# Low parts of the projection weights on VectorE instead of GpSimd, in two stages of a hybrid decoder block

## The chip, the cores and the metric

The kernel runs on one core of one Trainium2 chip. The metric is the device time of one execution in microseconds (us), the median of several runs. Besides, one execution is profiled: its trace has every instruction of the five engines, TensorE (PE; its weight loads are listed apart as PEld), VectorE (DVE), ScalarE (ACT), GpSimd (POOL) and SyncE (SP, which issues most DMAs).

## The reference, cut to what matters

One layer of a decoder block on 1024 tokens behind 16 learned ones, model width 1024, in float32:

```python
u = rmsnorm(h, norm1_w[l]) @ w_in[l]
(a_q, a_k, a_v, a_gate, a_b, a_a, b_z, b_xbc, b_dt, c_q, c_k, c_v, gate_logits) = split_in(u)
y_gdn = gdn_branch(a_q, a_k, a_v, a_gate, a_b, a_a, ...)   # gated delta rule, 8 heads of 128
y_ssd = ssd_branch(b_z, b_xbc, b_dt, ...)                  # state space, 4 groups, chunks of 128
y_swa = swa_branch(c_q, c_k, c_v, swa_sinks[l])            # windowed attention
merged = g_a * (y_gdn @ w_proj_gdn[l]) + g_b * (y_ssd @ w_proj_ssd[l]) + g_c * (y_swa @ w_proj_swa[l])
h = h + merged @ w_out[l]
h = h + jnp.square(jax.nn.relu(rmsnorm(h, norm2_w[l]) @ w_up[l])) @ w_down[l]
```

`q`, `k`, `v` of the delta net and `x`, `b`, `c` of the state space pass a short causal convolution along the tokens and a SiLU. The delta net then solves a triangular system in each chunk and carries a state from chunk to chunk.

## The kernel before, in words

**Numbers in two parts.** A float32 operand of a large product is split into a high part, a copy rounded to the type `fp32r`, and a low part, the difference of the number and its high part. A product is three passes over the contraction: high by high, high by low, low by high.

**A projection.** `proj` (line 174) computes 128 columns of `w_in` against all tokens. `split_w` (line 119) gets the weight tile: a DMA on SyncE's queue brings 128x1024 numbers into `wr`; ScalarE copies them into `wh` (line 124); GpSimd subtracts, `wl = wr - wh` (line 126, one instruction on 128x1024). `gemm` then runs, for each of two or three chunks of tokens, eight products `wh` by `hnh`, eight `wh` by `hnl` and eight `wl` by `hnh` (line 150). So `wl` is needed only in the last third of a chunk. `wr`, `wh` and `wl` have two buffers each: the tile for one projection is made while the one before it is multiplied, and it can be written only when the product two tiles earlier is over. In the trace `wl` bears the projection's name: `kl`, `vl`, `ql`, `ggl` in the delta net, `xl`, `zl`, `bl`, `cl` in the state space.

**The stages.** `stage_norm` (to about 32 us), `stage_gdn` (the delta net, to 640 us, some 79 us for each of 8 heads), `stage_ssd` (the state space, to 1060 us, some 100 us for each of 4 groups), `stage_swa` (attention), then gates, the merge of the branches, the output projection and the MLP.

**What VectorE does in the delta net.** The convolution of `q`, `k`, `v` (one step on line 354, three on line 359, two closing ones on line 362 behind ScalarE's tanh); the solve, a chain of 62 short instructions in which `xt` (line 514) and `ub` (line 516) wait for each other; the scan over the chunks, where `rr` (line 591) feeds PE's `py` (line 597) and `S` (line 609) feeds PE's `ks` (line 589); and products with decay matrices (`dm` line 479, which PE's `qtp`, line 486, waits for, since `dm` frees a bank of PSUM; `w` line 443). In the state space: the same convolutions (its first step on line 356), `xd` (line 721), `sq` (line 807, ahead of PE's `sst`, line 809), `dms` (line 777).

**What GpSimd does besides `wl`.** Selections under a diagonal (`dm` line 426, `dms` line 680), products with decays (`kt` line 448, `qt` line 470, `xw` line 726, `x` by `z` line 797) and powers for norms (lines 421, 632, 814; the last, `sf`, goes to PE's `sfr`, line 819).

**What sets the order.** Each engine works through its own queue in order, and an instruction that waits holds all behind it. The order in the queues is fixed when the program is built, by a planner that takes, of the instructions it reckons ready on an engine, the one that stands earliest in the program. `weave` and `tick` put the steps of the previous head's scan between the products of a projection in the program's text.

Of the kernel before, what the change touches and what calls it, by code (L numbers as in the profile page):

```python
# [7 lines left out]
F32 = mybir.dt.float32  # L8
# [3 lines left out]
ALU = mybir.AluOpType  # L12
# [51 lines left out]
class Trunk:  # L64
    def __init__(self, ctx, tc, I, out):
        self.ctx, self.tc, self.nc, self.I, self.out = ctx, tc, tc.nc, I, out
        nc = self.nc
        self.const = ctx.enter_context(tc.tile_pool(name="const", bufs=1))
        self.wst = ctx.enter_context(tc.tile_pool(name="wst", bufs=2))
        self.dram = ctx.enter_context(tc.tile_pool(name="scr", bufs=1, space=DRAM))  # L70
        self.pmm = ctx.enter_context(tc.tile_pool(name="pmm", bufs=3, space=PSUM))
        self.pcr = ctx.enter_context(tc.tile_pool(name="pcr", bufs=3, space=PSUM))
        self.pbx = ExitStack()
        self.open_psum()
        self.co = None
        const = self.const
        self.ident = const.tile([P, P], F32, name="ident")
        make_identity(nc, self.ident)
        self.tri = const.tile([P, P], F32, name="tri")
        nc.gpsimd.memset(self.tri, 1.0)  # L80
        nc.gpsimd.affine_select(out=self.tri, in_=self.tri, compare_op=ALU.is_ge, fill=0.0,
                                base=0, pattern=[[1, P]], channel_multiplier=-1)
        self.ones = const.tile([P, 1], F32, name="ones")
        nc.gpsimd.memset(self.ones, 1.0)
        self.pneg = const.tile([P, 16], F32, name="pneg")
        nc.gpsimd.memset(self.pneg, -0.5)
        self.ppos = const.tile([P, 16], F32, name="ppos")
        nc.gpsimd.memset(self.ppos, 0.5)
        self.cols = const.tile([P, NCOL], F32, name="cols")
        nc.scalar.dma_start(self.cols, I["cols"])  # L90
        self.hnw = const.tile([P, 9], F32, name="hnw")
        nc.vector.tensor_scalar(self.hnw, self.cols[:, C_GNW:C_GNW + 9], 0.5, None, op0=ALU.mult)
        self.hdk = const.tile([P, 8], F32, name="hdk")
        nc.vector.tensor_scalar(self.hdk, self.cols[:, C_DSK:C_DSK + 8], 0.5, None, op0=ALU.mult)
        self.sink = const.tile([P, SH], F32, name="sink")
        nc.scalar.dma_start(self.sink, I["sinks"].broadcast_to([P, SH]))
        self.yd = [self.dram.tile([KT, P, SEQ], F32, name=f"yd{b}") for b in range(3)]
        self.gad = self.dram.tile([3 * KT, P, SEQ], F32, name="gad")
        self.acd = self.dram.tile([NPR, 7, P, 512], F32, name="acd")
        self.xd = self.dram.tile([HOIST, P, 512], F32, name="xd")  # L100
        self.hd = self.dram.tile([NB, P, D], F32, name="hd")
        self.rowd = self.dram.tile([32, NC, P], F32, name="rowd")
        self.ald = self.dram.tile([32, NC], F32, name="ald")
        self.frd = self.dram.tile([SG, NB, P], F32, name="frd")
# [14 lines left out]
    def split_w(self, src, name):  # L119
        nc = self.nc  # L120
        wr = self.wst.tile([P, KT, P], F32, name=name + "r", tag="wr")
        nc.sync.dma_start(wr.rearrange("p k c -> p (k c)"), src)
        wh = self.wst.tile([P, KT, P], F32R, name=name + "h", tag="wh")
        nc.scalar.activation(wh, wr, AF.Copy)  # L124
        wl = self.wst.tile([P, KT, P], F32R, name=name + "l", tag="wl")
        nc.gpsimd.tensor_tensor(wl, wr, wh.bitcast(F32), op=ALU.subtract)  # L126
        return wh, wl

    def half(self, tag, bufs, name, dt=F32R, pool=None):
# [1516 lines left out]
def build(ctx, tc, I, out):  # L1646
    k = Trunk(ctx, tc, I, out)
    nc = tc.nc
    pool = lambda st, name, **kw: st.enter_context(tc.tile_pool(name=name, **{"bufs": 1, **kw}))
    ph, ps, px = ExitStack(), ExitStack(), ExitStack()  # L1650
    k.px = ExitStack()
    k.pa = ExitStack()
    with nc.allow_non_contiguous_dma(reason="layout"):
        k.tp = pool(ctx, "tp")
        k.hn = pool(ph, "hn", side="right")
        k.c2 = pool(k.pa, "c2")
        k.sp = pool(ps, "smp", side="right")
        k.xp = pool(px, "xp", side="right", bufs=3)
        k.stage_norm()
        px.close()  # L1660
        k.open_branches()
        cur = k.gdn_first()
        k.stage_small()
        ps.close()
        k.open_gdn()
        k.stage_gdn(cur)
        k.open_rest()
        k.stage_ssd()
        k.open_psum()
        store = k.stage_swa()  # L1670
        k.gates = {}
        k.merge_gates(0, (0, 1))
        w2 = k.gate_w(0, 2)
        store()
        k.px.close()
        k.pa.close()
        k.pbx.close()
        k.pdr = pool(ctx, "pdr", space=PSUM, reuse_waits="tile")
        k.lp = pool(ctx, "lp", reuse_waits="tile")
        k.ph, k.py = ph, ExitStack()  # L1680
        k.stage_merge(w2)
        k.py.close()
        k.rp = pool(ctx, "rp", side="right", reuse_waits="tile")
        k.stage_out()
        k.stage_mlp()
    return k
# [73 lines left out]
```

## Time and profile before

| | us |
|---|---|
| median of 3 runs | 2650.71 (2644.99 to 2651.49) |
| the profiled execution | 2650.12 |
| its span, first to last instruction | 2648.40 |
| busy in the span: PE | 2507.6 (95%) |
| VectorE | 1754.3 (66%) |
| ScalarE | 1071.5 (40%) |
| GpSimd | 572.2 (22%) |

A busy PE is not PE at its peak, since its instructions are pipelined and their ends modelled. "PEclk" in the tables is the clock that PE was granted, as a share of 2.4 GHz. In an instruction's row the number behind the start is its duration; the brackets say how long its engine was idle before it and what ended that. Several like instructions in a row are merged (x2, x8).

### The profile page before, as it was taken

What the parts mean: (1) busy time and instruction counts of PE and PEld (TensorE: products, weight loads), DVE (VectorE), ACT (ScalarE), POOL (GpSimd) and SP (SyncE); (2) the same over time, 40 slices, a digit from 0 to 9 for tenths busy, and PEclk for the clock granted to TensorE, in tenths of its full rate; (3) what the DMA queues carried; (4) which work ended last, traced back from release to release, by engine and by line L of the source; (5) the groups of instructions that cost most, each with busy time, mean ns of one, the idle gap of its engine ahead of it and who ended that gap; (6) DMA issues with size and microseconds to landing.
All of it is one profiled execution on the core that took longest, in us unless ns stands there. A gap on an engine that the chain in (4) does not pass through costs nothing.

```text
span 2648.4 us, 37818 instructions
## 1 busy us (share of the span) xinstructions
PE 2507.6 (95%) x13863; PEld 2142.1 (81%) x13863; DVE 1754.3 (66%) x3267; ACT 1071.5 (40%) x2647; POOL 572.2 (22%) x471
## 2 busy tenths in 40 slices
PE   6999999999999999999998999999999999999998
PEld 5887888888888989878887887888877788878886
DVE  5786678677457656567777754454537777686878
ACT  4334444343423323356554433221246454444443
POOL 3322222222223323321220000222341000041230
PEclk9999899999999999999999999999999999999999
DMA  3211111111111121231211334544234544666422
GB/s 117 74 37 54 54 54 54 46 53 41 61 62 59 65 77 67 62 84 49 69 61 64 134 109 136 187 159 159 92 116 155 198 166 149 214 232 206 147 87 97
DMA packets 136952, 271.84 MB, mean 103 GB/s; under 512 B 41302, under 2 KB 41718, under 8 KB 136766
## 3 DMA queue, kind: packets, MB, share of 16 engines
q1 hardware_dynamic: 131214, 256.94, 28.9%
q0 software_dynamic: 4544, 11.14, 1.7%
q8 instruction: 109, 1.79, 0.3%
q10 hardware_dynamic: 1008, 1.34, 0.2%
q14 instruction: 77, 0.63, 0.1%
HBM read 196.34 MB, written 66.59 MB: 99 GB/s over the span
## 4 chain that ended last, share of the span: by engine, by line
PE 72%; DVE 18%; issue 3%; DMA 3%; ACT 2%; POOL 1%; SPq 0%; ACTq 0%; DVEq 0%; POOLq 0%
PE dn L1540 10%; PE pr L1183 9%; PE up L1345 9%; PE gp L1103 7%; PE pso L1247 3%; PE aq L150 3%; PE x L150 3%; PE gg L150 3%; PE q L150 2%; PE v L150 2%; DVE xt L514 2%; PE z L150 2%; PE b L150 2%; PE k L150 2%; PE c L150 2%
## 5 line engine op out<-in xcount | busy, mean ns | idle before, releaser
L1540 PE MATMUL dn<-wh,ah 128*128 128x512 f32 x448 | 175.3, 391 | 4.3 <-ACT wh L1285 4.3
L1540 PE MATMUL dn<-wl,ah 128*128 128x512 f32 x448 | 175.2, 391 | 0.6 <-POOL wl L1286 0.6
L1540 PE MATMUL dn<-wh,al 128*128 128x512 f32 x448 | 175.0, 391 | 0.0
L1183 PE MATMUL pr<-yh,wph 128*128 128x512 f32 x384 | 150.2, 392 | 5.2 <-ACT yh L137 5.2
L126 POOL TENSOR_TENSOR wpl<-wpr,wph 128x1024 fp32r<-128x1024 f32 x24 | 60.0, 2501 | 420.4 <-PE gp L1103 215.3
L1183 PE MATMUL pr<-yl,wph 128*128 128x512 f32 x384 | 150.4, 393 | 0.0
L1183 PE MATMUL pr<-yh,wpl 128*128 128x512 f32 x384 | 149.8, 391 | 0.0
L1286 DVE TENSOR_TENSOR al<-ar,ah 128x512 fp32r<-128x512 f32 x112 | 99.0, 887 | 41.5 <-ACT ah L1285 41.3
L1285 ACT ACTIVATE ah<-ar 128x512 fp32r<-128x512 f32 x112 | 70.3, 627 | 108.2 <-PE dn L1540 80.8
L1286 POOL TENSOR_TENSOR wl<-wd,wh 128x512 fp32r<-128x512 f32 x48 | 71.8, 1501 | 193.3 <-ACT wh L1285 73.2
L1540 PEld LDWEIGHTS dn<-wh,ah 128*128 128x128 f32 x448 | 84.6, 189 | 22.5 <-ACT wh L1285 4.8
L1540 PEld LDWEIGHTS dn<-wl,ah 128*128 128x128 f32 x448 | 84.6, 189 | 18.6 <-POOL wl L1286 1.1
L1540 PEld LDWEIGHTS dn<-wh,al 128*128 128x128 f32 x448 | 84.5, 189 | 17.5
L1183 PEld LDWEIGHTS pr<-yh,wph 128*128 128x128 f32 x384 | 71.8, 187 | 23.2 <-ACT yh L137 7.4
L1183 PEld LDWEIGHTS pr<-yl,wph 128*128 128x128 f32 x384 | 72.0, 187 | 18.4 <-DVE yl L138 2.6
L1183 PEld LDWEIGHTS pr<-yh,wpl 128*128 128x128 f32 x384 | 72.0, 188 | 15.4
L124 ACT ACTIVATE wph<-wpr 128x1024 fp32r<-128x1024 f32 x24 | 25.4, 1060 | 142.5 <-PE pr L1183 130.6
L514 DVE TENSOR_TENSOR xt<-lb,ub 99x84 f32<-99x84 f32 (+23 forms) x248 | 78.4, 316 | 5.5
L1359 ACT ACTIVATE c<-c 128x512 f32<-128x512 f32 x64 | 40.3, 630 | 96.3 <-DVE c L1431 44.3
L1193 DVE SCALAR_TENSOR_TENSOR gt<-gt,pr 128x512 f32<-128x512 f32 x32 | 21.8, 687 | 81.4 <-PE pr L1183 81.3
L1345 PE MATMUL up<-uh,sh 128*128 128x512 f32 x256 | 69.8, 395 | 3.5 <-ACT sh L1285 3.5
L1345 PE MATMUL up<-ul,sh 128*128 128x512 f32 x256 | 70.2, 396 | 0.0
(549 smaller groups left out, 7273.0 us busy)
## 6 DMA issues: line engine op xcount, KB each, us to landing
ar<-acd SPq DMA_DIRECT2D x106, 256.0 KB
wu<-in_wup SPq DMA_DIRECT2D x37, 512.0 KB
acd<-s SPq DMA_DIRECT2D x64, 256.0 KB
gad<-gt SPq DMA_DIRECT2D x48, 256.0 KB
wpr<-in_wpr SPq DMA_DIRECT2D x24, 512.0 KB
yr<-yd SPq DMA_DIRECT2D x48, 256.0 KB
gt<-gad SPq DMA_DIRECT2D x48, 256.0 KB
acd<-c SPq DMA_DIRECT2D x48, 256.0 KB
```

The costliest lines, as they stand in the source:

```text
L124: nc.scalar.activation(wh, wr, AF.Copy)
L126: nc.gpsimd.tensor_tensor(wl, wr, wh.bitcast(F32), op=ALU.subtract)
L150: nc.tensor.matmul(ps[:, 0:n], a[:, k, :], b[k][:, c0:c0 + n], start=(i == 0 and k == 0), stop=(i == 2 and k == KT - 1))
L514: nc.vector.tensor_tensor(tv, lb[:, j:j + 1, j + 1:32].broadcast_to([3 * n_, n, m]), ub[:, 0:n, j:j + 1].broadcast_to([3 * n_, n, m]), op= ...
L1103: nc.tensor.matmul(ps, w[x][:, k * P:(k + 1) * P], self.go[p, k][y], start=(j == 0 and k == 0), stop=(j == 2 and k == 3))
L1183: nc.tensor.matmul(ps, x[:, k, :], y, start=(k == 0 and j == 0), stop=(k == KT - 1 and j == 2))
L1247: nc.tensor.matmul(ps, x[k, th][:, ts], y, start=(k == 0 and j == 0), stop=(k == KT - 1 and j == 2))
L1285: nc.scalar.activation(hi, src, AF.Copy)
L1286: (eng or nc.vector).tensor_tensor(lo, src, hi.bitcast(F32), op=ALU.subtract)
L1345: self.nc.tensor.matmul(ps, x[:, k * P:(k + 1) * P], ops[k][y], start=(j == 0 and k == 0), stop=(j == 2 and k == 3))
L1359: self.nc.scalar.activation(dst, src, AF.Relu)
L1540: nc.tensor.matmul(acc[t], x[:, t * P:(t + 1) * P], y, start=(i == 0 and m == 0), stop=(i == n - 1 and m == 2))
```

## The change

In the delta net and the state space (and in the first tiles, which are split in the stage of the norm) `wl` is computed by VectorE, in two instructions of 128x512, instead of by GpSimd in one of 128x1024. A flag, set when the kernel object is made and cleared ahead of `stage_swa`, chooses; from the attention on, `split_w` is as before. GpSimd keeps everything else.

```diff
@@ __init__
         self.co = None
+        self.vlo = True
@@ split_w
         wl = self.wst.tile([P, KT, P], F32R, name=name + "l", tag="wl")
-        nc.gpsimd.tensor_tensor(wl, wr, wh.bitcast(F32), op=ALU.subtract)
+        if self.vlo:
+            for k in (0, 4):
+                nc.vector.tensor_tensor(wl[:, k:k + 4, :], wr[:, k:k + 4, :], wh[:, k:k + 4, :].bitcast(F32), op=ALU.subtract)
+        else:
+            nc.gpsimd.tensor_tensor(wl, wr, wh.bitcast(F32), op=ALU.subtract)
         return wh, wl
@@ build
         k.stage_ssd()
         k.open_psum()
+        k.vlo = False
         store = k.stage_swa()
```

## Rows read from the trace of the kernel before

**Rows 1.** The page, part 4: the chain that ended last, by engine.

```profile
PE 72%; DVE 18%; issue 3%; DMA 3%; ACT 2%; POOL 1%; SPq 0%; ACTq 0%; DVEq 0%; POOLq 0%
```

**Rows 2.** Busy time of each engine by stretch (us and instructions), PE clock, DMA share, GB/s.

```profile
32.00:640.00 608.00, 562.20 (x3948) 506.01 (x3949) 422.51 (x991) 247.75 (x795) 158.75 (x111) 0.96 0.18 53
...
640.00:1060.00 420.00, 397.99 (x2518) 362.98 (x2517) 271.16 (x349) 139.81 (x348) 124.93 (x76) 0.98 0.18 63
...
1060.00:2648.40 1588.40, 1536.95 (x7353) 1264.45 (x7351) 1043.08 (x1906) 666.41 (x1478) 276.16 (x267) 0.99 0.39 131
```

**Rows 3.** PE's waits, 0 to 1060 us: total us, times, longest.

```profile
PE py L597 <- DVE rr L591: 19.3, 10, 2.6
...
PE qtp L486 <- DVE dm L479: 11.6, 5, 2.9
...
PE sst L809 <- DVE sq L807: 4.7, 3, 1.6
...
PE xtp L381 <- DVE x L362: 3.2, 2, 1.7
...
PE sfr L819 <- POOL sf L814: 3.2, 3, 1.4
```

**Rows 4.** GpSimd in order of time, 440 to 520 us: start, duration, instruction, [idle before].

```profile
474.84 2.38 POOL L126 TENSOR_TENSOR kl<-kr,kh 128x1024 fp32r<-128x1024 f32 x1 [11.03 <-PE psn L604]
...
513.46 1.56 POOL L426 TENSOR_SCALAR_AFFINE_SELECT dm<-gm 128x1024 f32<-128x1024 f32 x1
```

**Rows 5.** GpSimd in order of time, 488 to 512 us.

```profile
491.41 2.38 POOL L126 TENSOR_TENSOR vl<-vr,vh 128x1024 fp32r<-128x1024 f32 x1 [14.18 <-ACT sqo L618]
...
511.14 2.37 POOL L126 TENSOR_TENSOR ggl<-ggr,ggh 128x1024 fp32r<-128x1024 f32 x1 [0.34 <-PE k L150]
```

**Rows 6.** VectorE in order of time, 489 to 512 us.

```profile
491.53 2.36 DVE L514 TENSOR_TENSOR xt<-lb,ub 99x80 f32<-99x80 f32 x1
...
494.20 0.23 DVE L514 TENSOR_TENSOR xt<-lb,ub 99x72 f32<-99x72 f32 x1
...
494.62 0.76 DVE L354 TENSOR_SCALAR q<-qraw,cols 128x1040 f32<-128x1040 f32 x1
...
498.12 1.29 DVE L359 SCALAR_TENSOR_TENSOR q<-qraw,cols,q 128x1040 f32<-128x1040 f32 x1
...
511.53 2.53 DVE L354 TENSOR_SCALAR k<-kraw,cols 128x1040 f32<-128x1040 f32 x1
```

**Rows 7.** PE in order of time, 495 to 506 us.

```profile
499.87 0.49 PE L597 MATMUL py<-rr,w 128*128 128x128 f32 x2 [2.64 <-DVE rr L591]
```

**Rows 8.** Groups of instructions: count, busy us, mean ns, idle before.

```profile
L1286 DVE TENSOR_TENSOR wl<-T,wh 128x512 fp32r<-128x512 f32 x32 | 21.9, 684 | 6.4 <-PE dn L1540 5.9
...
L138 DVE TENSOR_TENSOR yl<-yr,yh 128x512 fp32r<-128x512 f32 x48 | 40.6, 866 | 30.0 <-ACT yh L137 29.9
...
L1286 DVE TENSOR_TENSOR wul<-wu,wuh 128x1024 fp32r<-128x1024 f32 x16 | 19.6, 1223 | 29.2 <-ACT wuh L1285 29.2
```

**Rows 9.** VectorE in order of time, 440 to 520 us.

```profile
474.87 0.35 DVE L609 SCALAR_TENSOR_TENSOR S<-S,egl,psn 128x128 f32<-128x128 f32 x1 [2.61 <-PE psn L604]
...
514.10 2.02 DVE L359 SCALAR_TENSOR_TENSOR k<-kraw,cols,k 128x1040 f32<-128x1040 f32 x1
```

**Rows 10.** VectorE in order of time, 900 to 965 us.

```profile
923.96 2.48 DVE L356 TENSOR_SCALAR x<-xraw,cols 128x1040 f32<-128x1040 f32 x1 [3.80 <-issue]
...
931.51 1.30 DVE L362 SCALAR_TENSOR_TENSOR x<-xth,x 128x528 f32<-128x528 f32 x2
...
954.62 0.82 DVE L356 TENSOR_SCALAR x<-xraw,cols 128x1040 f32<-128x1040 f32 x1 [1.04 <-DMA yd<-x]
...
960.17 2.70 DVE L362 SCALAR_TENSOR_TENSOR x<-xth,x 128x528 f32<-128x528 f32 x2 [0.71 <-ACT xth L361]
```

**Rows 11.** Busy time by stretch, around a fall of the clock.

```profile
925.00:935.00 10.00, 8.46 (x59) 8.18 (x58) 9.44 (x9) 4.78 (x10) 0.99 (x2) 1.00 0.17 54
...
935.40:945.60 10.20, 9.30 (x36) 8.85 (x36) 0.98 (x3) 0.73 (x2) 1.64 (x1) 0.50 0.08 31
```

## The prediction

> **What bounds the kernel now.** I read the chain that ended last first: TensorE (PE) has 72% of it, VectorE (DVE) 18% [rows 1]. So only what PE waits for, or what slows PE, can move the time. Then the sums by stretch: the change touches the delta net (32 to 640 us) and the state space stage (640 to 1060 us). There PE is busy 562.2 of 608 and 398.0 of 420 us; 45.8 + 22.0 = 67.8 us are idle. Its granted clock averages 0.96 and 0.98 of full speed [rows 2], which is 0.04 x 608 + 0.02 x 420 = 33 us lost at the lower clock. About 68 + 33 = 101 us is thus what this change could touch; the other 1588 us of the span keep their code.
>
> The waits of PE show who makes the idle time [rows 3]: nearly all of it ends with a VectorE instruction (the scan's right-hand side `rr` 19.3 us in 10 waits, `dm` 11.6 in 5, `sq` 4.7 in 3, the conv's last step `x` 3.2 in 2). No wait of PE in the two stages names a low part of a weight (line 126). GpSimd (POOL) makes them early enough; making them sooner is worth nothing. What can pay is what the subtraction does to VectorE.
>
> That is seen in the two engines' instructions in order of time. A subtraction on GpSimd, `kl` for one, takes 2.38 us [rows 4]. In one head of the steady state `vl` runs from 491.41 for 2.38 us [rows 5]; VectorE's `xt` that starts 0.12 us later takes 2.36 us, where the same instruction with 72 columns takes 0.23 [rows 6]. Both end together: VectorE stood for 2.13 us. `ggl` from 511.14 [rows 5] does the same to the conv's first step: 2.53 us [rows 6], against 0.76 for that instruction alone. Reading on: the conv's third weighted step runs from 498.12 [rows 6], `rr` comes behind it, and PE starts `py`, which needs `rr`, at 499.87 after 2.64 us of idle time [rows 7]. A good part of that gap is the 2.13 us that VectorE lost 6 us earlier in one unbroken run of work.
>
> **The change, part by part.** `split_w` is called 8 x 4 times for the heads and 4 x 6 times for the groups: 56 weight tiles go from GpSimd to VectorE. The switch is set back ahead of the attention stage, so 40 tiles stay as they are. No DMA moves; ScalarE's copies stay.
>
> Added to VectorE: 56 x 2 instructions of 128x512. That form exists later in the kernel, 0.684 us each with nothing beside it [rows 8], so 1.37 us a tile, 56 x 1.37 = 77 us in all.
>
> Removed from VectorE: the standing. Per head: `vl` 2.13, `ggl` 2.53 - 0.76 = 1.77; `ql` meets the same first step of the conv of `v` (I take 1.8 as for `ggl`); `kl` at 474.84 [rows 4] meets instructions that are not held up: `S` beside it takes 0.35 [rows 9]. Together 5.7 us a head against 4 x 1.37 = 5.5 us added. In a group: the first step of a conv takes 2.48 where it takes 0.82 alone, 1.66 lost; the two last steps of `x` take 2.70 where two such take 1.30 alone, 1.4 lost [rows 10]. At 1.4 a tile the six tiles lose 8.4 us against 8.2 added. Over both stages: 8 x 5.7 + 4 x 8.4 = 79 us removed, 77 added. VectorE's load does not change; what changes is when it stands and in what pieces: a piece of 2.4 us that nothing can pass becomes two of 0.68, and the queue's order is made knowing of them.
>
> What follows for PE's gaps, each with its two ends:
> - `py` behind `rr`, 10 waits, 19.3 us [rows 3]. Before, 2.13 stands ahead of `rr`. If both halves of the subtraction come ahead of it, 2.13 - 1.37 = 0.76 is won; if none does, 2.13, but no more than the gap. The low parts stand later in the program than the solve, the conv and the scan around them, so that they are filled in where nothing earlier is ready; often one half will come first. The short ones of the ten have less to give: I take 0.8 for each, 8 us (5 to 17).
> - `qtp` behind `dm`, 5 waits, 11.6 us. Before, the conv ahead of it loses 1.77 to `ggl` and 2.02 - 1.30 = 0.72 to GpSimd's `dm` selection, which queued behind `ggl` [rows 4, 6, 9]. With `ggl` gone that selection (1.56 us) moves up and may hold up the conv's start instead. So 2.49 becomes 1.37 + 0 to 1.56: from -0.4 to +1.1, and +2 where the halves come later. I take 0.6, 3 us (-2 to 9).
> - `sst` behind `sq`, 3 waits, and `xtp` behind the conv, 2 waits. 1.66 and 1.4 become 1.37 or less: 0.3 to 1.6 and 0 to 1.4. I take 0.7 each, 4 us with rounding (1 to 8).
> - Other short waits behind VectorE in these stages: 1 us (0 to 2).
>
> Together 16 us of idle time (4 to 36). The clock: after a stretch of 10 us in which PE was idle for 1.5 at full clock, 935.4 to 945.6 is granted 0.50 of full speed, 1.2 of 2.4 GHz [rows 11]; 10.2 us there do some 5 us of work. With a quarter of the idle time gone (16 of 68) I take a quarter of the 33 us: 8 us (0 to 16).
>
> What it costs: VectorE's new work where nothing was held up before, `kl` above all: 8 x 1.37 = 11 us of VectorE. At 474.84 VectorE had waited 2.61 us for PE [rows 9], so this mostly fills idle time; if that cover is gone, the scan's `S` and `rr` come 1.37 us later and PE waits. I take 3 us (0 to 11). GpSimd's shorter queue lets its other work start sooner; I count that at nothing except in the second line above. A low part that comes a few microseconds later is counted at nothing: PE waits for none now [rows 3], and if that cover is gone its waits will name the new line.
>
> Sum against the profiled execution, 2650.12 us (span 2648.40 and 1.72 around it; the median of the runs is 2650.71, 0.6 above, so they are alike): 2650.1 - 16 - 8 + 3 = 2629.
>
> One thing speaks against the sum: VectorE is busy 422.5 of 608 us in the delta net [rows 2], 69%, and GpSimd 159. If the standing that I count as removed is no gain, 77 us of work come to VectorE, and by its share of the chain (18%) [rows 1] 14 us to the time: 2664 (a rival below). The Trainium skill (Perfetto Trace Analysis, Optimizing Scalar/DVE Operations) has the rule: work may go from a saturated DVE to GpSimd, the reverse of this change; it adds that with the SBUF port they share this may not help. The 2.36 us `xt` agrees with the second half.
>
> **The rivals.**
> *Traded one for one* (about no change): all halves come ahead of whatever PE waits for, since they become ready just before the conv that they used to hold up (`ggl` 511.14, the conv's step 511.53) [rows 5, 6]. Then the idle time gives little more than its low end, 6 us, the clock nothing, and `kl` costs 4: about 2648. For it: the two sums, 79 and 77, are equal. Against it: the gaps hang on 2.13 us and 1.66 us pieces, and these shrink in any order.
>
> *VectorE waits at the head of its queue* (slower): a subtraction needs ScalarE's copy and a low buffer that PE has finished with. On GpSimd that wait harmed nobody; on VectorE the solve chain, `S`, `rr` and the conv queue behind it. The price is seen where VectorE makes low parts today: it stood 30.0 us ahead of 48 such instructions for the merge (0.63 each) and 29.2 ahead of 16 in the up projection (1.83 each) [rows 8]. At 1.2 a tile, 67 us, half of it in runs that PE waits for: +34 against -21, so 2663. It decides from 0.75 us a tile on (half of 56 x 0.75 is 21). Against it: the release is PE's last product of a projection, and the conv that follows waits for the same moment anyway; the 1.83 belongs to a stage with little else in the queue.
>
> *The block turns round*: VectorE's halves hold up what GpSimd keeps. Its `sf` is one step ahead of PE's `sfr` (3.2 us in 3 waits [rows 3]), and it makes such powers 8 + 8 + 4 times; 20 x 0.68 = 14 us less gain, about 2643. The Trainium skill (SBUF — State Buffer, Who interferes with whom) has the rule: whichever of the two starts first keeps the port for its whole instruction. The rows show only the direction in which GpSimd was first.
>
> *The load counts* (slower): the 77 us without the standing, 2664, as above. Against it: the standing is in the rows, instruction by instruction.
>
> *Gains in full*: most halves fall into idle slots, and the clock follows. 31 + 16 us off, about 2603.
>
> That the change does not do what it says can be left out: one line makes the low part, and the flag is set before the first tile.
>
> **How the numbers follow.** Forecast, 2629 with its own range 2615 to 2642: 0.50. Traded one for one, 2648: 0.20. VectorE waits at its head, 2663: 0.10. The load counts, 2664: 0.03. Turned round, 2643: 0.08. In full, 2603: 0.09. A change under 0.3% (8 us) cannot be told from none here. Faster by more: 0.50 + 0.09 + half of 0.08 + 0.03 of the trade = 0.66; within: 0.21; slower: 0.13. The range 2604 to 2656 leaves out the two slower rivals and half of the full gain, 0.18.
>
> **What would show it.** Right: in the delta net `xt` and the conv's first steps (lines 354, 356) lose their instructions above 2 us except beside GpSimd's `qt`, `dm`, `xw`; VectorE's busy time in 32 to 1060 stays within some 10 us of 693.7; PE's waits for `rr` fall from 19.3 to about 11 and for `dm` from 11.6 to about 9; the clock averages 0.97 to 0.98 in the delta net. Wrong: VectorE idle ahead of the new instructions with ScalarE or PE as releaser by more than 0.75 us a tile; or PE's waits for `rr`, `S` and `dm` unchanged in sum; or GpSimd's powers later than now. The later stages should keep their time to within 2 us; if they don't, the reason isn't in this sum.

## The result and the profile after

The change makes the kernel faster: 2601.16 us (median of 4 runs) against 2650.0 (also 4) of the kernel before, a ratio of 0.9817 with a 95% interval of 0.9801 to 0.9833, 49 us. The direction was forecast, the size was not: 2629 was predicted, and 2601 lies below the low end of the range, 2604. All ratios leave out executions at a much lower granted clock: one of experiment 4, the profiled one of experiment 9 (0.745), whose trace is therefore not read, and one of the kernel before.

The page of the kernel after, part 1 (busy us, share of the span, instructions); its profiled execution took 2595.83 us, span 2594.1:

```profile
PE 2494.0 (96%) x13863; PEld 2131.3 (82%) x13863; DVE 1743.5 (67%) x3379; ACT 1069.5 (41%) x2647; POOL 448.3 (17%) x415
```

VectorE took over 112 instructions, whose durations add up to 77 us, and is busy 11 us less than before; GpSimd is busy 124 us less. Where the time went is read up to the first product of the attention, at 1075.60 us before and 1024.40 after. Busy time by stretch of before (us, PE, PEld, DVE, ACT, POOL, PE clock, DMA share, GB/s):

```profile
0.00:1075.60 1075.60, 984.52 (x6577) 888.50 (x6577) 718.87 (x1371) 409.79 (x1177) 301.36 (x207) 0.97 0.19 60
```

and of after:

```profile
0.00:1024.40 1024.40, 969.91 (x6576) 876.88 (x6576) 709.55 (x1483) 407.90 (x1177) 177.10 (x151) 0.98 0.20 64
```

51.2 us are gone here. PE's idle time fell from 91.1 to 54.5 (36.6), its busy time by 14.6 with the same instructions. The busy part is the clock: the stretches granted 0.50 of full speed add up to 75 us before and 44 after, and half of that difference is 15. The later stages gave 3 us. The clock differs between executions: the profiled one had a mean of 0.986, the other three 0.978 to 0.984; so in the median the clock gives some 5 us less than in this trace, about 10.

VectorE's busy time tells of the standing. In experiment 1 below GpSimd's subtraction is gone and VectorE does nothing in its place; there VectorE is busy, in the same part of the program:

```profile
0.00:1016.40 1016.40, 963.32 (x6576) 871.13 (x6576) 648.69 (x1371) 408.39 (x1177) 224.64 (x207) 0.99 0.21 64
```

So 718.9 - 648.7 = 70 us of standing are gone, and the halves add 709.6 - 648.7 = 61 us to the busy time. That is less than their 77, since in the trace an instruction can start shortly before the one ahead has ended (the half at 389.80 below lasts to 390.48, the next instruction starts at 390.40). The instructions that stood in [rows 6, 10] are now short. Groups of instructions of after (count, busy us, mean ns, idle before):

```profile
L359 DVE TENSOR_SCALAR k<-kraw,cols 128x1040 f32<-128x1040 f32 x8 | 6.3, 786 | 0.6 <-PE ks L594 0.6
...
L361 DVE TENSOR_SCALAR x<-xraw,cols 128x1040 f32<-128x1040 f32 x8 | 6.5, 818 | 4.8 <-DMA yd<-x 4.8
```

These are the conv's first steps, lines 354 and 356 of before (behind `split_w` the lines of after are 5 higher; those of the experiments differ by 0 to 2 more). PE's waits of after, 0 to 1060 us (total us, times, longest), which answer to [rows 3]:

```profile
PE xps L223 <- DVE xn L218: 18.9, 3, 17.1
PE py L602 <- DVE xt L519: 5.2, 3, 1.7
PE sfr L824 <- POOL sf L819: 4.2, 3, 1.4
...
PE qtp L491 <- DVE dm L484: 3.6, 5, 0.8
PE py L602 <- DVE ub L521: 3.3, 2, 1.8
PE xtp L386 <- DVE x L367: 2.1, 3, 1.6
...
PE py L602 <- DVE rr L596: 1.8, 6, 0.4
```

`py` waits 10.3 us in all instead of 19.3, `qtp` 3.6 instead of 11.6, `sst` for `sq` is no longer in the list. Of what is left of `py`, 8.5 us stand behind `xt` and `ub`: there GpSimd's `qt`, a product that the change leaves on it, holds VectorE. One of five such places in the kernel after, all engines in order of time:

```profile
473.68 2.37 POOL L475 TENSOR_TENSOR qt<-qt,q 128x1024 f32<-128x1024 f32 x1 [2.45 <-DVE q L367]
...
473.90 2.22 DVE L521 TENSOR_TENSOR ub<-ub,xt 99x54 f32<-99x54 f32 x1
...
477.02 0.46 PE L602 MATMUL py<-rr,w 128*128 128x128 f32 x2 [1.72 <-DVE xt L519]
```

An `ub` of this size takes 0.21 us elsewhere; 0.22 us behind the start of `qt` it takes 2.22, and both end within 0.07 us of each other.

Most of this waiting is new. In the kernel before only two of `py`'s ten waits stand behind `qt`, 1.58 us at 504.83 and one of 0.12; the other 17.6 us stand behind low parts, and all but 1.8 of those are gone. So the change took 16 us of `py`'s waits away and brought 7 new ones behind `qt`. VectorE stood beside `qt` in the other heads of before as well (2.21 us instead of 0.20 at 424.24), but in three of the four that later wait, PE was then at the lower of its two clock levels and had work throughout. Busy time beside `qt` in such a head and in the one that waited:

```profile
423.40:426.80 3.40, 3.40 (x15) 3.40 (x16) 3.33 (x6) 0.54 (x3) 2.37 (x1) 0.50 0.00 0
...
501.60:504.80 3.20, 1.66 (x12) 1.37 (x10) 3.13 (x7) 1.00 (x4) 2.37 (x1) 1.00 0.00 0
```

and in the kernel after, where all five are at full clock:

```profile
473.70:477.00 3.30, 1.60 (x11) 1.33 (x10) 3.20 (x7) 0.65 (x3) 2.35 (x1) 1.00 0.37 139
```

So part of what the clock gave back, PE lost again by waiting at full speed. What lowered the clock there is not shown: both heads had the same gap of `py` (2.65 us) shortly ahead.

**One gap, followed through four kernels.** The gap of `py` behind `rr` that the prediction costed is best seen in one head, between PE's `ks` and `py`. Before, all engines in order of time:

```profile
413.93 2.36 DVE L514 TENSOR_TENSOR xt<-lb,ub 99x80 f32<-99x80 f32 x1
...
414.15 0.38 PE L589 MATMUL ks<-S,k 128*128 128x128 f32 x2
...
417.02 0.76 DVE L354 TENSOR_SCALAR q<-qraw,cols 128x1040 f32<-128x1040 f32 x1
...
421.87 0.35 DVE L591 SCALAR_TENSOR_TENSOR rr<-ks,neg,vt 128x128 f32<-128x128 f32 x1
...
422.27 0.38 PE L597 MATMUL py<-rr,w 128*128 128x128 f32 x1 [2.65 <-DVE rr L591]
```

After, in the same head:

```profile
389.69 0.38 PE L594 MATMUL ks<-S,k 128*128 128x128 f32 x2
...
389.80 0.68 DVE L129 TENSOR_TENSOR vl<-vr,vh 128x512 fp32r<-128x512 f32 x1
...
390.56 0.75 DVE L359 TENSOR_SCALAR q<-qraw,cols 128x1040 f32<-128x1040 f32 x1
...
395.44 0.34 DVE L596 SCALAR_TENSOR_TENSOR rr<-ks,neg,vt 128x128 f32<-128x128 f32 x1
...
395.83 0.68 DVE L129 TENSOR_TENSOR vl<-vr,vh 128x512 fp32r<-128x512 f32 x1
...
395.84 0.38 PE L602 MATMUL py<-rr,w 128*128 128x128 f32 x1 [0.36 <-DVE rr L596]
```

One half stands ahead of the conv, the other behind `rr`. From `ks` to `py` it takes 6.15 us instead of 8.12, 1.97 less; but the gap fell by 2.29. The missing 0.3 us is in PE's own queue. Products of the projection `k` alone between the two, PE busy and count, before:

```profile
414.55:422.20 7.65, 5.07 (x32) 4.78 (x31) 1.00 0.20 71
```

and after:

```profile
390.10:395.80 5.70, 5.38 (x34) 5.09 (x33) 1.00 0.01 3
```

Two products more, 0.16 us each, stand ahead of `py`. So the order of PE's queue is another one with the new work on VectorE. That is taken up again with experiments 1 and 4.

### The profile page after: what moved, and what is told of

Read it like the earlier page. It is cut to its first block, busy times and chain, and to the rows that moved or that the text cites. A ratio compares the mean times of both kernels' runs of the same rounds, so it can differ in the third digit from the quotient of the medians.

```text
span 2594.1 us, 37914 instructions
## 1 busy us (share of the span) xinstructions
PE 2494.0 (96%) x13863; PEld 2131.3 (82%) x13863; DVE 1743.5 (67%) x3379; ACT 1069.5 (41%) x2647; POOL 448.3 (17%) x415
## 5 line engine op out<-in xcount | busy, mean ns | idle before, releaser
L1350 PE MATMUL up<-uh,sl 128*128 128x512 f32 x256 | 69.7, 394 | 0.0
```

Source lines behind the costliest of these rows:

```text
L1350: self.nc.tensor.matmul(ps, x[:, k * P:(k + 1) * P], ops[k][y], start=(j == 0 and k == 0), stop=(j == 2 and k == 3))
```

## The experiments

The diffs are against the kernel after unless another is named. Ratios are to the kernel before, with their 95% interval in brackets.

**1. No low part at all: the standing and the work both gone.** GpSimd only writes zeros.

```diff
-            for k in (0, 4):
-                nc.vector.tensor_tensor(wl[:, k:k + 4, :], wr[:, k:k + 4, :], wh[:, k:k + 4, :].bitcast(F32), op=ALU.subtract)
+            nc.gpsimd.memset(wl.bitcast(F32), 0.0)
```

> The low parts of the 56 tiles are left out of the computation: GpSimd fills them with zeros, which reads nothing, and VectorE gets no new work. Theory S (what the change wins is the time in which VectorE stood beside GpSimd's reads; the new work fits into VectorE's idle time): like the changed kernel or a little faster, 2590 to 2602. Rival W (the new work costs, and only the standing pays more than it): clearly faster than the changed kernel, 2575 to 2588. Rival O (the order in which the planner put VectorE's instructions pays, not the standing): the order falls back to that of before, 2625 to 2650.

Measured: 2593.75 us, 0.9783 [0.9761, 0.9805]. The whole of GpSimd's subtraction cost 57 us; giving it to VectorE keeps 49 of them. In the head shown above, all engines in order of time:

```profile
381.93 0.38 PE L593 MATMUL ks<-S,k 128*128 128x128 f32 x2
...
387.93 0.38 PE L601 MATMUL py<-rr,w 128*128 128x128 f32 x1 [0.53 <-DVE rr L595]
```

and the products of `k` between the two:

```profile
382.33:387.90 5.57, 5.07 (x32) 4.78 (x31) 1.00 0.21 82
```

The 32 products are the same as before, so the queue's order did not move; `py` comes 2.12 us sooner behind `ks`, and the gap shrinks by 2.12. That is the 2.13 us of the stalled `xt`, to a hundredth. The time is within the 2590 to 2602 of the theory that the standing is what the change wins.

**2. Standing and work together, in the delta net only.** Before, with VectorE besides subtracting two pieces of 432 columns into a spare tile, for 30 of the tiles; the diff is against before and cut to the lines in `split_w`; the others make the spare tile and set it for the delta net.

```diff
+        if self.spare is not None:
+            for c in (0, 512):
+                nc.vector.tensor_tensor(self.spare, wr.rearrange("p k c -> p (k c)")[:, c:c + 432],
+                                        wh.rearrange("p k c -> p (k c)")[:, c:c + 432].bitcast(F32), op=ALU.subtract)
```

> GpSimd subtracts as before, and VectorE besides subtracts 2 x 432 of the 1024 columns into a spare tile, in the delta net from the second projection pair on (30 tiles). Nothing of the computation is left out. Theory S: the standing is back and work is added, so as before or slower, 2648 to 2665. Rival O (order pays): VectorE's queue is laid out as in the changed kernel, so some of the gain comes, 2625 to 2640. If the added work costs nothing at all: 2650.

Measured: 2672.63, 1.0076 [1.0055, 1.0098]. On top of the standing, even part of the work makes the kernel 20 us slower, more than the 2665 that was expected at most. It isn't a pure price of work: some of the added pieces stood beside GpSimd themselves (those of `ql` took 1.25 us in the mean, those of `vl` 0.60). Experiment 12 does it in full.

**3. One piece instead of two halves.**

```diff
-            for k in (0, 4):
-                nc.vector.tensor_tensor(wl[:, k:k + 4, :], wr[:, k:k + 4, :], wh[:, k:k + 4, :].bitcast(F32), op=ALU.subtract)
+            nc.vector.tensor_tensor(wl, wr, wh.bitcast(F32), op=ALU.subtract)
```

> The changed kernel with one VectorE instruction of 128x1024 (1.22 us) instead of two of 128x512. Theory S: the pieces matter little, 2600 to 2608. Rival H (the halves pay, since one is put ahead of the conv and the other behind the scan's step): 0.55 us more ahead of the scan's step and of the selection in each head, up to 10 us and the clock, 2612 to 2625.

Measured: 2595.58, 0.9796 [0.9767, 0.9825], a little below the 2600 to 2608 expected; the piece takes 1.22 us. The interval overlaps that of the kernel after: that the halves are two is worth nothing that shows. In the head shown above the piece stands ahead of the conv, 38 products stand ahead of `py`, and its gap is 0.48.

**4. The halves at the head of the planner's order.**

```diff
+            with self.tc.high_priority():
                 for k in (0, 4):
                     nc.vector.tensor_tensor(wl[:, k:k + 4, :], wr[:, k:k + 4, :], wh[:, k:k + 4, :].bitcast(F32), op=ALU.subtract)
```

> The changed kernel with both halves given the planner's high priority, so that they come as soon as their inputs are there, ahead of the conv, the scan and the solve. Theory S: 0.68 us more in front of what PE waits for, twice a head and a group, about 15 us if all of it counts, 2603 to 2618. Rival O (order pays): most of the gain goes, 2635 to 2650.

Measured: 2609.67, 0.9828 [0.9797, 0.986], not to be told from the kernel after. Both halves now come ahead of the conv and `rr`, the case for which the prediction had `py` win only 0.76 us. All engines in order of time, in the same head:

```profile
397.91 0.38 PE L595 MATMUL ks<-S,k 128*128 128x128 f32 x2
...
398.24 1.28 DVE L130 TENSOR_TENSOR vl<-vr,vh 128x512 fp32r<-128x512 f32 x2
...
404.88 0.38 PE L603 MATMUL py<-rr,w 128*128 128x128 f32 x1 [0.55 <-DVE rr L597]
```

and the products of `k` between the two:

```profile
398.31:404.80 6.49, 6.02 (x38) 5.74 (x37) 1.00 0.24 83
```

From `ks` to `py` it takes 6.97 us, 1.15 less than before, near the 0.76. But the gap is 0.55, 2.10 less: 38 products stand ahead of `py` now, six more, 0.95 us, and 1.15 + 0.95 is the 2.10. So a half ahead of `rr` does delay it, and PE's queue has more work ahead of `py` by as much. The two heads that follow, at 499.87 and 579.06 us of before, repeat this: gaps of 2.64 us in both before, 0.37 and 0.35 after, 0.51 and 0.53 in experiment 1, 0.55 in both here, behind 32, 34, 32 and 38 products.

**5. GpSimd busy as before, but without reading.** Three times zeros.

```diff
-            for k in (0, 4):
-                nc.vector.tensor_tensor(wl[:, k:k + 4, :], wr[:, k:k + 4, :], wh[:, k:k + 4, :].bitcast(F32), op=ALU.subtract)
+            for _ in range(3):
+                nc.gpsimd.memset(wl.bitcast(F32), 0.0)
```

> As the run without low parts (56 tiles' low parts left out), but GpSimd fills each tile with zeros three times, so that it is busy for some 2.9 us a tile where the subtraction took 2.4, and reads nothing. If the standing of VectorE comes from GpSimd's reads of two inputs (theory S): as the run without low parts, 2588 to 2602. If it is GpSimd's being busy that costs, since its other work queues behind the subtraction (rival G): back to 2640 to 2655.

Measured: 2595.94, 0.9784 [0.9761, 0.9807], the same as experiment 1, with GpSimd busier than in the kernel before (page, part 1):

```profile
PE 2492.5 (96%) x13863; PEld 2130.2 (82%) x13863; DVE 1685.9 (65%) x3267; ACT 1070.8 (41%) x2647; POOL 609.6 (23%) x583
```

So neither GpSimd's load nor its queue mattered, only that it reads. The Trainium skill (SBUF — State Buffer, Who interferes with whom) has the rule: a VectorE instruction with two SBUF inputs contends with a GpSimd instruction that reads SBUF, not with one that only writes. The two ratios, 0.9784 and 0.9783, agree. The conv's first step, which has one input in SBUF, is a little longer beside the fills. Its group for `k`, 786 ns in the kernel after:

```profile
L359 DVE TENSOR_SCALAR k<-kraw,cols 128x1040 f32<-128x1040 f32 x8 | 8.4, 1056 | 14.4 <-ACT kraw L355 14.4
```

Over all these first steps that is 43 us instead of 34.

**6. Each half twice: 77 us more of counted work.**

```diff
-            for k in (0, 4):
+            for k in (0, 4, 0, 4):
```

> The changed kernel with each half subtracted twice: 77 us more work for VectorE, known to the planner that lays out the queues. Theory P (work that the planner counts is laid into gaps, standing it does not know of is not): about as cheap as the first 77 us, 8 to 15 us, 2606 to 2618. Rival L (VectorE has slack only since the standing is gone, and more work uses it up): half of it counts, as where work was added on top of the standing, 2630 to 2650.

Measured: 2608.82, 0.9834 [0.9814, 0.9853]. Another 77 us of VectorE (61 of busy time) cost some 5 us (0.9834 - 0.9817), and the two intervals overlap. The load is not the limit.

**7. Two halves on GpSimd, nothing on VectorE.**

```diff
-                nc.vector.tensor_tensor(wl[:, k:k + 4, :], wr[:, k:k + 4, :], wh[:, k:k + 4, :].bitcast(F32), op=ALU.subtract)
+                nc.gpsimd.tensor_tensor(wl[:, k:k + 4, :], wr[:, k:k + 4, :], wh[:, k:k + 4, :].bitcast(F32), op=ALU.subtract)
```

> The kernel before with GpSimd's subtraction in two instructions of 128x512, nothing moved to VectorE. Theories S and P: the sum of the standing is the same, 2640 to 2655. Rival H (a long piece that nothing can pass is what costs): 2615 to 2635.

Measured: 2641.2, 0.9967 [0.9948, 0.9987], in ten runs between 2633 and 2654. Standing in pieces half as long is worth 9 us, a fifth of what the change brings. The halves take 1.28 to 1.59 us in the mean.

**8. Four more products of GpSimd moved to VectorE**: `qt` (in two halves), `kt`, `xw` and `x` by `z`. One of the four, the others alike:

```diff
-        nc.gpsimd.tensor_tensor(kt, kt, ktc.unsqueeze(2).broadcast_to([P, NC, P]), op=ALU.mult)
+        nc.vector.tensor_tensor(kt, kt, ktc.unsqueeze(2).broadcast_to([P, NC, P]), op=ALU.mult)
```

> The changed kernel with four more of GpSimd's products with two SBUF inputs moved to VectorE in the two stages (q by its decay in two halves, k, x and x by z whole; 32 in all, 1.2 to 1.4 us each). Theories S and P: some 35 to 40 us of standing go and 40 us of counted work come, at the prices of the runs so far (0.8 and 0.12 a us) 20 to 28 us faster than the changed kernel, 2572 to 2585. Rival L: the load is traded, 2595 to 2610.

Measured: 2579.42, 0.9724 [0.9706, 0.9743]; the interval doesn't meet that of the kernel after. The gap behind `qt` is gone; all that is left of `py`'s wait in PE's list (0 to 1007 us):

```profile
PE py L603 <- DVE rr L597: 1.1, 3, 0.4
```

Busy time up to the attention's first product: VectorE's is below that of the kernel after, 709.6, though it has those products too:

```profile
0.00:1007.30 1007.30, 966.02 (x6576) 874.34 (x6576) 701.45 (x1521) 408.12 (x1177) 99.36 (x121) 0.98 0.20 65
```

**9. The kernel after, with GpSimd's reads put back** behind the halves, into `wr`, which nobody uses any more.

```diff
                 nc.vector.tensor_tensor(wl[:, k:k + 4, :], wr[:, k:k + 4, :], wh[:, k:k + 4, :].bitcast(F32), op=ALU.subtract)
+            nc.gpsimd.tensor_tensor(wr, wr, wh.bitcast(F32), op=ALU.subtract)
```

> The changed kernel, and behind VectorE's two halves GpSimd subtracts once more, in place, into the tile that holds the raw weights, whose content nobody reads any more; the result is unchanged. So the 56 GpSimd instructions of some 2.4 us that read two inputs are back, with nothing moved from VectorE. Theory P (standing that the planner does not count falls on PE, counted work does not): against the same base where 77 us of counted VectorE work cost 5 us, this standing of up to 56 x 1.4 = 78 us costs 30 to 55 us, 2630 to 2655. Rival L (any delay of VectorE is now covered by its slack): like the doubled halves, 2604 to 2615.

Measured: 2693.5, 1.0141 [1.0108, 1.0174], where at most 2655 was expected. `wr` is also kept longer than in the kernel after, which may be part of the price; experiment 12 tries the same corner in the other order.

**10 and 11. Experiment 8 with more low parts on VectorE**: the attention's 12 tiles (10), and those of the gates and the merge too, 28 (11, where the last line of this diff is missing as well).

```diff
-        k.vlo = False
         store = k.stage_swa()
         k.gates = {}
+        k.vlo = False
```

> The kernel with the four products moved as well, and the 12 weight tiles of the attention stage split on VectorE too. Theory P: their standing (0.8 us for each of 12 on the trace of before, 10 us) goes where PE waits for VectorE: 0 to 8 us less than the kernel with the four products, 2571 to 2580. Rival T (attention's VectorE work is denser, so that counted work costs too): 2580 to 2590.

> As the run before it, with the gates' and the merge's weight tiles on VectorE as well (28 more). In the merge PE is busy 98% of the stretch and waits for no one, so that theory P expects nothing there although GpSimd holds VectorE up by some 40 us on the trace of before: the same as the run before it within 4 us, 2568 to 2580. If standing counts wherever it is: 2535 to 2555.

Measured: 2577.93, 0.9696 [0.9654, 0.9738], and 2574.07, 0.9699 [0.9672, 0.9725]. Neither can be told from experiment 8 or from the other with certainty; the fastest of the series lie at 2574 to 2579 us.

**12. The missing corner: GpSimd subtracts as before, then VectorE's halves write the same numbers again, all 56 tiles.**

```diff
         if self.vlo:
+            nc.gpsimd.tensor_tensor(wl, wr, wh.bitcast(F32), op=ALU.subtract)
             for k in (0, 4):
                 nc.vector.tensor_tensor(wl[:, k:k + 4, :], wr[:, k:k + 4, :], wh[:, k:k + 4, :].bitcast(F32), op=ALU.subtract)
```

> The fourth corner of a square: for all 56 tiles GpSimd subtracts as before, and VectorE then writes the same low part again in two halves, which wait for GpSimd's. Nothing is left out. If counted work costs the same with and without the standing (theory P alone, prices add): 2653 + 9 = 2660, 2655 to 2668. If work on top of the standing costs more, as where VectorE wrote into a spare tile in the delta net (20 us for 30 tiles): 2675 to 2695. If the halves, by coming later than the copy by ScalarE, take part of the standing into waits that VectorE has anyway: 2635 to 2655.

Measured: 2690.1, 1.0147 [1.0106, 1.0187]. With this the square of standing and work is full:

| | VectorE's halves: no | yes |
|---|---|---|
| GpSimd reads: no | 0.9783 (1) | 0.9817 (after) |
| GpSimd reads: yes | 1 (before) | 1.0147 (12) |

The same 77 us of work cost 0.0034, 9 us, where GpSimd doesn't read (the two intervals overlap slightly), and 0.0147, 39 us, where it does. The same reads cost 57 us without the work and 87 with it; experiment 9 gave 86 for the same step (1.0141 - 0.9817). That the two prices simply add (2660) is refuted. The corners are not quite one change apart: in (1) GpSimd fills with zeros, and in (12) VectorE's halves come behind GpSimd's tile and not beside it.

Busy time up to the attention's first product:

```profile
0.00:1115.00 1115.00, 1009.84 (x6576) 910.67 (x6576) 783.22 (x1483) 410.35 (x1177) 318.56 (x207) 0.94 0.19 58
```

Against before, PE is idle 14 us more (105.2) and busy 25 us more; its stretches at 0.50 add up to 126 us instead of 75, and half of that difference is the 25. VectorE's busy time, 783, is 3 above the 719 of before and the 61 that the halves add: there is hardly more standing in sum. I read the rest as work that finds no free time where it falls, with the clock behind it; that is argued, not shown. The halves themselves are held up in part, as these groups of instructions show (mean 1040 against 680 ns); for GpSimd's tile ahead of them VectorE waits 4.0 us in all:

```profile
L130 DVE TENSOR_TENSOR zl<-zr,zh 128x512 fp32r<-128x512 f32 x16 | 16.3, 1040 | 1.7 <-POOL zl L128 1.7
...
L130 DVE TENSOR_TENSOR kl<-kr,kh 128x512 fp32r<-128x512 f32 x16 | 10.9, 680 | 0.0
```

## Why the prediction fell short, point by point

**The mechanism was right.** VectorE stood while GpSimd read, PE waited for that, and both ends of it are in the rows. Experiments 1 and 5 show it from two sides: the reads are the cause, not GpSimd's load. The forecast that VectorE's busy time would stay within 10 us came out at 9 less (up to the attention); the clock in 32 to 640 us rose from 0.96 [rows 2] to 0.97, as forecast. The chain of waits of after is followed over 39% of the span only, so it isn't set beside [rows 1].

**The step that failed: charging the halves against the standing, one for one.** The prediction took 79 us of standing off VectorE, put 77 of work on it, and let PE's gaps win the difference at each place: 2.13 - 1.37 = 0.76 at `py`. The time from `ks` to `py` behaves nearly so (1.15 less in experiment 4, with both halves ahead). But the gap isn't that time. The prediction held the products ahead of `py` for fixed; in the three heads compared there are 32, 34 or 38 of them, with none, one or two halves in front. Work that stands in the program moves PE's order, and PE has something to do meanwhile; the standing, which isn't in the program, moved nothing and fell on PE in full: 2.12 of 2.13 us in experiment 1. So nearly the whole gap goes there, however the halves lie. That the count of products follows the halves is shown; that the planner reckons with the work and not with the standing is how I read it, and was not looked into. Nor does all standing fall on PE: behind `qt` it fell there for more than 0.2 us in one head of before and in five of after.

By its terms, in us of the profiled execution:

| term | taken | measured |
|---|---|---|
| `py` | 8 (5 to 17) | 9.0: 16 off, 7 new behind `qt` |
| `qtp` | 3 (-2 to 9) | 8.0 |
| `sst` and `xtp` | 4 (1 to 8) | 7.6 |
| first tiles, 0 to 96 us before | not in the sum | 4.9 |
| other short waits | 1 (0 to 2) | 7.1, what is left of the 36.6 |
| clock | 8 (0 to 16) | 15, about 10 in the median |
| later stages | 0 | 3 |
| new work where nothing stood | -3 (-11 to 0) | not apart |

Three terms were mis-sized for the reason above. `qtp` lost 8.0 of 11.6 us; in the prediction a 1.37 us tile still stood in the 2.49 that went. `py` looks right by luck: the prediction read all ten waits as the low parts', though [rows 7] follows one only; of the 17.6 us that were theirs 16 went, twice the 8, and the 7 that came behind `qt` were counted at nothing. (`xtp` is 5.0 us before, its third wait being at the end of the stage.) The first tiles were left out though the diff sets the flag ahead of them: PE idles 21.7 us instead of 26.6 up to the first head's `kk`. The short waits were each too small to be read, and are together nearly as large as `qtp`. The later stages gave 3 us where the prediction allowed 2; why is not known.

**New work at 3 us.** The square gives it 9 us (0.9817 - 0.9783; the intervals overlap slightly, so it is not clear of noise), and experiment 6 some 5 for the next 77. Within its bounds of 0 to 11. It is cheap only when the standing has gone: in experiment 12 it cost 39.

**The rivals.** *Gains in full*, 2603 at a chance of 0.09, is what came in number: 31 us of idle time and 16 of clock there, 36.6 and 10 to 15 here. It had no sum by places, so this does not show that the halves fell into idle slots. *Traded one for one* rested on 79 against 77; in VectorE's busy time it is 70 against 61, so the near equality was right, and it didn't decide. *VectorE waits at the head of its queue* had its condition fulfilled and still failed. The idle time of VectorE ahead of the halves in the kernel after, by who ended it:

```profile
  ACT zh L125: 20.5, 5
  PE k L155: 16.2, 5
  PE z L155: 12.9, 3
  PE gg L155: 11.7, 6
```

In all 87 us, 1.56 a tile, twice the 0.75 from which it was to decide. But apart from those behind `qt`, no wait of PE for VectorE grew by more than about 1 us: what stood behind the halves in the queue can hardly have been what PE needed next. Such idle time prices a move only with the name of the one who waits for what comes next. *The load counts*: refuted by experiment 6. *The block turns round* is there, and small. In the kernel after, GpSimd's selection, 1.56 us in [rows 4], and a power that took 1.64 before:

```profile
486.02 2.17 POOL L431 TENSOR_SCALAR_AFFINE_SELECT dm<-gm 128x1024 f32<-128x1024 f32 x1 [2.28 <-PE po L620]
...
494.27 2.01 POOL L637 TENSOR_TENSOR f<-f,pneg 128x8 f32<-128x8 f32 x1 [1.64 <-DVE f L635]
```

Only the power is a case of the rival: one of VectorE's halves, `ggl`, started 0.17 us ahead of it. The selection stands behind a step of the conv that started 0.07 us ahead. The powers that PE waits for next, `sf`, take 1.64 us in both kernels; PE's wait for them went from 3.2 to 4.2 us all the same, 1 us where 14 were feared.

**What stays open.** How the extra 30 us of experiment 12 divide between halves held up, `wr` kept longer, order and clock. And a delay of VectorE that isn't in the program, made without GpSimd, was not tried; that it would fall on PE as the standing does is argued, not shown. Nor is it shown what lowered the clock at each place.

## What to carry to other kernels

When work leaves an engine that makes another stand, don't set the work against the standing one for one: ask which of the two the order of the queues was made with. Here PE's order moved with the work, which was mostly covered, and not with the standing, which landed on the bottleneck. An instruction that takes ten times as long as its like, and ends together with one of GpSimd, is the sign; its excess is inside VectorE's busy time, so a share of 66% here held some 70 us of standing that went away. A stall that seems to cost nothing may be covered only by a bottleneck at half clock, as `qt`'s was. Idle time ahead of a new instruction is no price until a wait of the bottleneck names what stands behind it.

## What the runs showed of the hardware

GpSimd's reads hold VectorE up to their end, instructions with two inputs in SBUF (`xt`, 2.36 us instead of 0.23) and the conv's first step with one (2.53 instead of 0.76). Its fills lengthen that first step (1.06 instead of 0.79 in the mean for `k`); 168 of them (experiment 5) cost no more than 56 (experiment 1), where 56 subtractions cost 57 us. The Trainium skill (Perfetto Trace Analysis, Optimizing Scalar/DVE Operations) says of moving work between the two that it might not help, for the port that they share; here the move from GpSimd to VectorE gave 49 us, and with four more products 73 (experiment 8), while VectorE's busy time fell. And the clock went with PE's idle time in sum: 75 us at half speed beside 91 of idle time before, 44 beside 54 after, 126 beside 105 in experiment 12.
